# A list scheduler that prices each kind of small matrix product on its own, in a hybrid conformer, delta-net and feed-forward layer

## The chip, the cores and the metric

The kernel runs on one core of one Trainium2 chip. The metric is the device time of one execution in microseconds (us), less is better. A core has five engines that work side by side, each through its own instructions in a fixed order: TensorE (PE, matrix products into PSUM), VectorE (DVE), ScalarE (ACT), GpSimd (POOL) and SyncE (SP, which here issues all transfers).

## What is computed

The input has 512 tokens of width 1024, and 16 learned meta tokens go ahead of them. One layer and a last norm are computed, in float32:

```python
u = rmsnorm(h);  P = u @ w_in                       # one projection, columns shared out
c = silu(layernorm(causal_dwconv(c_val * sigmoid(c_gate), 31 taps)));  y_conf = c @ w_conf_out
q, k, v = silu(causal_dwconv(..., 4 taps)); q, k l2-normed    # 8 heads, width 128
o = chunk_gated_delta_rule(q, k, v, g, beta)        # state S per head, chunk by chunk
y_dn = (rmsnorm(o) * silu(z)) @ w_dn_out
h = h + (sigmoid(gA) * y_conf + sigmoid(gB) * y_dn) @ w_out
up = causal_dwconv(rmsnorm(h) @ w_up, 3 taps)
h = h + (silu(f_gate) * f_val) @ w_down             # d_ff 2816
return rmsnorm(h)[meta tokens dropped]
```

The delta rule needs, for each head and each chunk of 128 tokens, the inverse of a unit triangular 128x128 matrix.

## The kernel before

Features lie on partitions, tokens along the free dimension, in two halves of 258 or 264 columns. Each weight tile (wr, 128x1024) is split into a rounded part (wh, by ACT) and the rest (wl, by DVE), and so is each activation; a product of the full matrices is then three passes of fp32r products of 128x128 by 258, 264 or 512 columns. These are called big products here. A big product of 258 columns starts every 0.12 us.

Beside them stand small products in plain fp32, which the array takes as tiles of less than 128x128. The kinds are: 128x32 (`rs`, `sums`: sums over partitions, four token groups on four column groups), 32x32 and 64x64 (`gP` and `gX` in `grow`: the inverses of 32-blocks grow to 64 and 128), 32x128 and others for the 16 meta tokens. Full-width fp32 products of 128 columns do the chain of the state: `kS`, `wP`, `S` and `o`, four chunks per head in `heads`. Between these the chain runs over DVE (`r`, the new state `S`) and ACT (`w`).

DVE also does the 31-tap convolution of the conformer (`ca`, 240 steps) and the 32-block inverses; ACT empties most of PSUM.

No order is written out by hand. `record` notes every engine call with the tiles that it touches, and `Plan.order` puts the calls in a row: a list scheduler with a clock for each engine, which always takes the engine that can start first and gives it the ready call of the lowest number. The number is the place in the program, moved by `BIAS` and a few other constants for each stage. The time that a call is thought to take comes from `price`, the handover between engines from `LAT`. Each engine then keeps that order on the chip; where the planner's durations are off, an engine waits. Two lines matter most. A small product that does not begin at partition 0 of PSUM was priced at its issue alone, and leaving small products for others cost the number `STAY`, but only towards a product that is not small:

```python
            if out.ap.offset // out.tl.row:
                return 22, 0
...
                if e == "PE" and part and not o.part:
                    p += STAY
```

So the planner saw no cost in taking small products of different kinds in turn. Every recorded call carries one line in the profile, L427, since one helper issues all of them; groups are told apart by tile names.

Of the kernel before, what the change touches and what calls it, by code (L numbers as in the profile page):

```python
# [12 lines left out]
F32R = mybir.dt.float32r  # L13
# [6 lines left out]
P = 128  # L20
# [46 lines left out]
class Vw:  # L67
    """a view of a tile: the steps to it, and the same steps taken on a stand-in to know its bounds"""
# [52 lines left out]
class Op:  # L121
    _fields = ("eng", "fn", "a", "k", "prio", "deps", "succ", "late", "wait", "cost", "ready", "end", "tiles", "lat", "table")
# [11 lines left out]
TABLES = {'Exp': ('exp',), 'Tanh': ('exp', 'silu'), 'Silu': ('silu',), 'Sqrt': ('sqrt',)}  # L134
LAT = {'PE': {'PE': 3, 'DVE': 200, 'ACT': 200, 'POOL': 200, 'SP': 200},
# [5 lines left out]
WIN = 3413.3  # L141
LOW = 0.4
HIGH = 0.84
# ---- the order: how far ahead of the first open call each engine looks, slots kept for the tile that is next in
# line, what it costs to leave a run of small products or to change a function table ----
AHEAD = {'PE': 3000, 'DVE': 3000, 'ACT': 3000, 'POOL': 400, 'SP': 400}
KEEP = {"p1": 1, "st": 1, "bt": 2}
STAY = 3000
SWITCH = 600
# [1 line left out]
BIAS = {'k3': -850, 'iv': -1500, 'd0': 150, 'v4': -30, 'v2': 0, 'd7': 1500, 'z1': -320, 't11': -280, 'z5': 0, 't7': 250, 'k0': -250, 'ln': 250, 's7': 30, 'z0': -700, 'o2': -250, 'o5': 100, 'd5': -1850, 'g3': 150, 'd6': -250, 'd1': 2130, 'k2': -30, 'q7': -1720, 'k5': -30, 's4': -730, 'd4': 850, 'w3': -1600, 't2': -600, 'c5': -130, 't8': 60, 'v3': 250, 'o4': -600, 'q6': -250, 'g4': -350, 't4': -100, 'o1': 250, 'q4': -630, 't9': -150, 'z2': -600, 'o0': -600, 'g0': 30, 'q3': 250, 'q5': 700, 'c1': 30, 'c6': -130, 's1': 0, 't15': 200, 't1': -700, 's3': 100, 'y0': 250, 't12': -150, 'o6': 100, 'o3': 250, 'k4': -100, 'w2': 250, 't5': -250, 'v0': 30}  # L151
LNP = 74
IVP = 1265
UP = 519
WP = 144
# [39 lines left out]
class Plan:  # L195
# [18 lines left out]
    def add(self, eng, fn, a, k):  # L214
# [27 lines left out]
        o.part = eng == "PE" and fn == "matmul" and (writes[0].shape[0] < P or args[1].shape[0] < P) and writes[0].shape[0] % 32 == 0  # L242
        o.share = args[1].shape[0] / P if o.part else 1.0
        o.cost, o.lat = self.price(eng, fn, a, k, writes[0])
        if eng == "ACT" and fn == "activation":
            o.table = TABLES.get(str(k["func"]).split(".")[-1])
        self.ops.append(o)

    def price(self, eng, fn, a, k, out):
        n = out.n  # L250
        if eng == "PE":
            lhs, rhs = (k["lhsT"], k["rhs"]) if fn == "matmul" else (a[1], a[2])
            n = rhs.n
            if fn == "transpose":
                return 110, 0
            # a tile of the array beside one that is busy costs its issue alone
            if out.ap.offset // out.tl.row:
                return 22, 0
            return max(n, lhs.n) / 2.4 * (1 if lhs.tl.dt == F32R else 4) + 3, 0
        if fn == "dma_start":  # L260
            runs = [v.ap.ap[-1][1] if v.ap.ap[-1][0] == 1 else 1 for v in (k["out"], k["in_"])]
            return 475, int(np.prod(out.shape)) * 4 / 360.0 * (1 if min(runs) > 127 else 2)
# [3 lines left out]
        if eng == "ACT":  # L266
            return 0.833 * n + (51 if any(v.tl.space == "psum" for v in src) else 93) + 93 * aps + 93 * ("accum_out" in k), 0
        if eng == "DVE":
            r = {"reciprocal": 6.3, "tensor_copy": 1.04 if psum else 0.52, "tensor_scalar": 1.04 if psum else 0.52}.get(fn, 1.042)
            return r * n + 65 + 62 * aps, 0  # L270
        return 1.0 * n + 80, 0

    def order(self):
        """list scheduling: the engine that can start first takes its ready call of the lowest number"""
# [17 lines left out]
        part, drain = False, 0.0  # L292
        # a memset waits until the call that it is for has one other thing to wait for
# [13 lines left out]
        def look(e, t):  # L307
            """the call to take at t, or the next moment when there may be one"""
            q, nxt, best = ready[e], later[e][0][0] if later[e] else None, None
            for p, i in q:  # L310
# [23 lines left out]
                if e == "PE" and not o.part:  # L334
                    st = max(st, drain)
# [3 lines left out]
                if e == "PE" and part and not o.part:  # L339
                    p += STAY  # L340
                elif o.table and table not in o.table:
                    p += SWITCH
# [4 lines left out]
        while len(out) < len(ops):  # L347
# [26 lines left out]
            if e == "PE":  # L374
                # the tensor engine's clock: full after a busy window, half after an idle one
                while t >= (win + 1) * WIN:
# [4 lines left out]
                    win, act = win + 1, 0.0  # L381
                if cold:
                    c *= 2
                act += c * o.share
                part, drain = o.part, t + c + 86 if o.part else 0.0
            free[e] = t + c
            o.end = free[e]
            if e == "SP":
                dma = max(dma, t + 1100) + o.lat
                o.end = dma + 950  # L390
# [4 lines left out]
            for v in o.tiles:  # L395
# [4 lines left out]
                if not v.left and v.tag in slots:  # L400
                    heapq.heappush(slots[v.tag], tend[v] + 100)
            for j in o.succ:
                s = ops[j]
                s.ready = max(s.ready, o.end + LAT[e][s.eng])
# [25 lines left out]
def record(A, out):  # L430
# [41 lines left out]
    def weights(src, n=D):  # L472
        """raw tile -> its 12-bit part and the exact rest"""
# [9 lines left out]
    def gemm(acc, ws, ah, al, ranges, k0=0, kn=None, first=True, last=True):  # L483
# [3 lines left out]
        if ah is uh and WHOLE:  # L487
            # not before all of its rows are there: it would hold its banks
# [12 lines left out]
    def sums(ss, width):  # L501
        """tiles [128, width]: sum over tiles and partitions, four token groups on partition groups"""
# [8 lines left out]
    def spread(r, width, n):  # L511
        """such rows on every partition of a tile in SBUF"""
# [9 lines left out]
    def rstd_rows(ss, width, scale, bias):  # L522
        """the sums' 1/sqrt(scale*sum+bias)"""
# [19 lines left out]
    # the first products take the input without its norm's scale, which comes after them  # L543
# [3 lines left out]
    # products of nothing while the first loads run: the tensor engine's clock is up when they are in  # L547
# [34 lines left out]
    # 32 columns: four k-tiles at a time, side by side in the array; their sums come with the turn to tokens  # L582
# [38 lines left out]
    # halves of the products below come doubled out of (tanh + 1)  # L621
# [35 lines left out]
    # beta = exp(min(b, 0)) / (1 + exp(-|b|))  # L657
# [9 lines left out]
    # cumulated decays: by token on partitions, by row, and the chunks' totals  # L667
# [47 lines left out]
    def conv4(acc, t, way=None):  # L715
        """four causal taps, then silu; from PSUM [128, 2, 268], or [128, 2, 264] moved out first, or SBUF"""
# [37 lines left out]
    def decays(h):  # L754
        """E[j, i] = exp(gc_i - gc_j) for j <= i, else 0"""
# [9 lines left out]
    def grams(h):  # L765
# [23 lines left out]
        # b = beta / (|k|^2 + eps)  # L789
# [22 lines left out]
    def inverses():  # L812
# [478 lines left out]
```

## Time and profile before

| | |
|---|---|
| median of 3 runs | 1048.68 us (1046.71 to 1049.07) |
| span of the profiled execution | 1049.7 us |
| PE busy | 1035.5 us, 99% |
| DVE busy | 718.3 us, 68% |
| ACT busy | 474.7 us, 45% |
| mean granted clock of PE | 0.985 of full |

The span reaches from the first to the last instruction of one profiled execution; what lies around it has no row, and the span is 1.0 us above the median of the runs. PE's busy share is high because its queue is rarely empty: a busy PE may still be working through products that are slow for their size, so the table alone doesn't tell how much time could go. The granted clock is 1.00 at 2.4 GHz and 0.50 at 1.2 GHz.

### The profile page before, as it was taken

Reading aid. Unit: us, or ns where it says so; the run is one execution under the profiler, and the core shown is the slowest. Engines: PE = TensorE matmul, PEld = TensorE weight load, DVE = VectorE, ACT = ScalarE, POOL = GpSimd, SP = SyncE. Lnnn points to the kernel's source line nnn. Section 1 sums busy time; section 2 is a strip of 40 time slices with the busy share of each in tenths; the row PEclk is TensorE's granted clock in tenths of the full one; section 3 lists DMA queues with packets and bytes.
Section 4 is the critical chain, followed back from the end, with each engine's and each line's share of the span. In section 5 each row is a group of like instructions: output and inputs, shape, how many; then the busy total and the mean of one; then the engine's idle time right before and its main releaser. Section 6 shows DMA issues by size and latency. Waiting matters only on the chain.

```text
span 1049.7 us, 20033 instructions
## 1 busy us (share of the span) xinstructions
PE 1035.5 (99%) x8430; PEld 985.7 (94%) x8430; DVE 718.3 (68%) x1237; ACT 474.7 (45%) x863; POOL 9.5 (1%) x45
## 2 busy tenths in 40 slices
PE   9999999999999999999999999999999999999996
PEld 7999999988989999999999999999999999988885
DVE  6987899984867998985546555666666767623324
ACT  6777622557534466444345234534444443413222
POOL 0011000000000000000000000000000000000000
PEclk9999999987999999999999999999999999999998
DMA  6244323231211232212313343232323232333232
GB/s 223 76 123 110 114 82 111 81 102 42 71 42 61 81 106 98 78 65 76 127 61 122 101 143 99 81 102 81 100 81 101 81 101 81 96 91 91 81 105 81
DMA packets 44042, 98.40 MB, mean 94 GB/s; under 512 B 12720, under 2 KB 19248, under 8 KB 43952
## 3 DMA queue, kind: packets, MB, share of 16 engines
q1 hardware_dynamic: 43952, 97.12, 29.2%
q8 instruction: 66, 1.08, 0.4%
q14 instruction: 24, 0.20, 0.1%
HBM read 93.89 MB, written 3.21 MB: 93 GB/s over the span
## 4 chain that ended last, share of the span: by engine, by line
PE 96%; DVE 1%; ACT 1%; DMA 0%; SPq 0%; issue 0%; POOL 0%; DVEq 0%; POOLq 0%; ACTq 0%
PE up L427 24%; PE dn L427 12%; PE ga L427 9%; PE y L427 9%; PE k L427 5%; PE v L427 5%; PE z L427 5%; PE q L427 4%; PE wo L427 4%; PE cv L427 4%; PE cg L427 4%; PE rs L427 2%; PE o L427 2%; PE gX L427 1%; PE S L427 1%; PE gP L427 1%
## 5 line engine op out<-in xcount | busy, mean ns | idle before, releaser
L427 DVE TENSOR_TENSOR wl<-wr,wh 128x1024 fp32r<-128x1024 f32 x157 | 189.3, 1207 | 160.1 <-PE dn L427 47.8
L427 ACT CAST wh<-wr 128x1024 fp32r<-128x1024 f32 x157 | 162.0, 1037 | 287.5 <-PE up L427 87.8
L427 DVE SCALAR_TENSOR_TENSOR ca<-c,par,ca 128x516 f32<-128x516 f32 (+10 forms) x240 | 177.3, 744 | 7.3 <-ACT ca L427 4.8
L427 PE MATMUL up<-hl,wh 128*128 128x258 f32 x704 | 142.1, 283 | 0.0
L427 PE MATMUL up<-hh,wh 128*128 128x258 f32 x704 | 142.1, 283 | 0.0
L427 PEld LDWEIGHTS up<-hh,wh 128*128 128x128 f32 x704 | 109.0, 190 | 0.2 <-issue 0.2
L427 PEld LDWEIGHTS up<-hl,wh 128*128 128x128 f32 x704 | 108.9, 189 | 0.0
L427 PE MATMUL up<-hh,wl 128*128 128x258 f32 x704 | 92.4, 283 | 0.0
L427 PEld LDWEIGHTS up<-hh,wl 128*128 128x128 f32 x704 | 88.3, 189 | 0.0
L427 DVE TENSOR_TENSOR up<-up,r 128x258 f32<-128x258 f32 x88 | 33.4, 420 | 49.0 <-PE up L427 46.0
L427 DVE SCALAR_TENSOR_TENSOR uy<-up,par,uy 128x512 f32<-128x512 f32 x88 | 65.9, 748 | 1.5
L427 PE MATMUL dn<-fh,wh 128*128 128x512 f32 (+1 forms) x198 | 65.0, 369 | 0.0
L427 PE MATMUL dn<-fl,wh 128*128 128x512 f32 (+1 forms) x198 | 64.9, 369 | 0.0
L427 ACT ACTIVATE uy<-up,par 128x512 f32<-128x512 f32 x44 | 36.0, 817 | 53.8 <-DVE up L427 53.8
L427 PE MATMUL ga<-uh,wh 128*128 128x258 f32 x256 | 58.5, 290 | 0.0
L427 PE MATMUL ga<-ul,wh 128*128 128x258 f32 x256 | 57.9, 289 | 0.0
L427 DVE SCALAR_TENSOR_TENSOR cv<-ra,par,cv 128x528 f32<-128x528 f32 x69 | 51.6, 760 | 0.6 <-ACT cv L427 0.5
L427 PE MATMUL dn<-fh,wl 128*128 128x512 f32 (+1 forms) x198 | 49.8, 370 | 0.0
L427 PE MATMUL ga<-uh,wl 128*128 128x258 f32 x256 | 48.4, 299 | 0.0
L427 PEld LDWEIGHTS dn<-fh,wh 128*128 128x128 f32 x198 | 36.9, 188 | 7.8 <-ACT wh L427 1.2
L427 PEld LDWEIGHTS dn<-fl,wh 128*128 128x128 f32 x198 | 36.9, 188 | 6.9
L427 PEld LDWEIGHTS ga<-ul,wh 128*128 128x128 f32 x256 | 42.2, 189 | 0.8 <-issue 0.6
(284 smaller groups left out, 2238.9 us busy)
## 6 DMA issues: line engine op xcount, KB each, us to landing
wr<-in_win SPq DMA_DIRECT2D x64, 512.0 KB, 3.3
wr<-in_wup SPq DMA_DIRECT2D x44, 512.0 KB, 3.7
wr<-in_wd SPq DMA_DIRECT2D x17, 512.0 KB, 3.6
wr<-in_wdn SPq DMA_DIRECT2D x8, 512.0 KB, 3.2
wr<-in_wco SPq DMA_DIRECT2D x8, 512.0 KB, 3.4
wr<-in_wo SPq DMA_DIRECT2D x8, 512.0 KB, 3.3
wr<-in_wd SPq DMA_DIRECT2D x8, 384.0 KB, 3.1
x<-in_xT SPq DMA_DIRECT2D x8, 264.0 KB, 5.8
```

The costliest lines, as they stand in the source:

```text
L427: getattr(engines[o.eng], o.fn)(*(get(x) for x in o.a), **{n: get(x) for n, x in o.k.items()})
```

## The change

The mathematics and the set of calls stay as they are; 7720 products on PE in both. What changes is the planner. A small product now has a kind (`mode`, rows by columns of the tile that it takes of the array). It pays `TURN` when the kind changes, in either direction and between two small kinds, and then its full cost as well. Leaving a kind costs `STAY` in number towards every other kind. Durations in `price` are new for most operations, transfers are thought slower, and what small products count for in the planner's own bookkeeping of PE's clock is new. `BIAS`, `LNP`, `IVP`, `WP` and `SWITCH` have other values, so the whole order is another. Comments are gone. The core of the diff:

```diff
-STAY = 3000
-SWITCH = 600
+STAY = 4687.5
+SWITCH = 300
...
+RATE = 0.4453
+TURN = {(False, True): 92, (True, False): 105, (True, True): 190}
...
-        o.part = eng == "PE" and fn == "matmul" and (writes[0].shape[0] < P or args[1].shape[0] < P) and writes[0].shape[0] % 32 == 0
+        o.mode = None
+        if eng == "PE" and fn == "matmul":
...
+            up = lambda n: 32 if n <= 32 else 64 if n <= 64 else P
+            o.mode = (up(args[1].shape[0]), up(writes[0].shape[0]))
+            o.mode = None if o.mode == (P, P) else o.mode
...
+        o.alone = self.price(eng, fn, a, k, writes[0], True)[0] if o.mode else o.cost
...
-            return max(n, lhs.n) / 2.4 * (1 if lhs.tl.dt == F32R else 4) + 3, 0
+            if lhs.tl.dt == F32R:
...
+                return RATE * n + 4 + (2 if rhs.ap.offset % rhs.tl.row % 4 else 0), 0
+            if lhs.shape[0] == 64:
+                return 115, 0
+            return max(n, lhs.n) / 0.6 + 8, 0
...
-                if e == "PE" and part and not o.part:
+                if e == "PE" and mode and o.mode != mode:
                     p += STAY
...
+                if o.mode != mode:
+                    c = o.alone + TURN[bool(mode), bool(o.mode)]
```

First place: PE in the middle of the delta rule, where `grow` for later heads and the head norms' sums come together (`gX` and `gP` are products of `grow`, `rs` with `hsel` are the sums of a head's squares `o` and `q`; `o_3`, `S_3` are products for the meta tokens). Before:

```order
L427 MATMUL S_3_3811<-w_6_3801,kdm_930 128x128
L427 MATMUL o_3_3813<-Em_1000,w_6_3801 128x16
L427 MATMUL gX_3817<-DU_2902,gp_3805 32x32
L427 MATMUL rs_3819<-o_1_3454,hsel_71 32x129
L427 MATMUL gX_3817<-DU_2902,gp_3805 32x32
L427 MATMUL rs_3819<-o_1_3454,hsel_71 32x129
L427 MATMUL gX_3817<-gp_3805,DU_2902 32x32
```

The same sums with the change:

```order
L447 MATMUL ga_3869<-uh_117,wl_3846 128x258 x2
L447 MATMUL ga_3869<-uh_125,wl_3846 128x258 x2
L447 MATMUL rs_3999<-o_1_3389,hsel_71 32x129 x4
L447 MATMUL rs_3999<-q_1_2775,hsel_71 32x129 x4
L447 MATMUL rs_3999<-o_2_3691,hsel_71 32x129 x4
L447 MATMUL rs_3999<-q_3_3632,hsel_71 32x129 x4
L447 MATMUL wP_4020<-r_9_3992,mn_1263 128x128
```

The sums stand in one run of 16 behind big products, and the products of `grow` in runs of their own elsewhere.

Second place: PE where the growth of the inverses begins (`ga` and `q` are big products). Before:

```order
L427 MATMUL ga_2915<-ul_121,wh_2850 128x258
L427 MATMUL gP_3002<-LL_2950,mn_1351 32x32 x5
L427 MATMUL gX_3028<-DU_2902,gp_3013 32x32
L427 MATMUL gP_3002<-LL_2950,mn_1351 32x32
L427 MATMUL gX_3028<-DU_2902,gp_3013 32x32
```

With the change:

```order
L447 MATMUL gP_2937<-LL_2912,mn_1225 32x32 x7
L447 MATMUL q_2947<-uh_93,wh_2845 128x264 x2
L447 MATMUL q_2947<-ul_95,wh_2845 128x264 x2
L447 MATMUL q_2947<-uh_97,wh_2845 128x264
L447 MATMUL gP_2983<-LL_2918,mn_1341 32x32 x8
L447 MATMUL q_2947<-uh_97,wh_2845 128x264
L447 MATMUL gX_2998<-DU_2843,gp_2977 32x32 x2
```

More big products stand between the first steps of the growth.

Third place: DVE at the end of the program (`fin` are output tiles, eight for each half of the tokens, `rr` is the norm's reciprocal, `xr` with `dn` the last residual). Before:

```order
L427 TENSOR_TENSOR fin_11675<-xr_7450,rb_11655 128x256
L427 TENSOR_TENSOR fin_11679<-xr_7452,rb_11655 128x256
L427 TENSOR_TENSOR fin_11679<-xr_7497,rb_11655 128x256
L427 RECIPROCAL rr_11668<-rr_11668 128x64
L427 TENSOR_TENSOR fin_11690<-xr_7020,rb_11685 128x256
```

With the change:

```order
L447 TENSOR_TENSOR fin_11653<-xr_7448,rb_11614 128x256
L447 TENSOR_TENSOR fin_11653<-xr_7496,rb_11614 128x256
L447 TENSOR_TENSOR xr_7496<-xr_7496,dn_11573 128x256
L447 RECIPROCAL rr_11682<-rr_11682 128x64
L447 TENSOR_TENSOR fin_11690<-xr_7322,rb_11685 128x256
```

The first half's eight output tiles now stand ahead of the last residual, and nothing stands between it and the second half's reciprocal. On PE 38 big products stand between the first half's `rb` and the end, where none stood.

## Rows read from the trace of the kernel before

**Rows 1.** The page: the span, and the chain that ended last by engine.

```profile
span 1049.7 us, 20033 instructions
...
PE 96%; DVE 1%; ACT 1%; DMA 0%; SPq 0%; issue 0%; POOL 0%; DVEq 0%; POOLq 0%; ACTq 0%
```

**Rows 2.** Windows: stretch, busy PE, PEld, DVE, ACT, POOL; granted clock; DMA.

```profile
98.00:112.00 14.00, 11.98 (x97) 11.20 (x96) 11.76 (x32) 11.54 (x52) 1.51 (x4) 1.00 0.46 97
112.00:224.00 112.00, 112.00 (x919) 110.96 (x919) 103.90 (x244) 41.59 (x68) 0.98 (x5) 1.00 0.34 103
224.00:263.00 39.00, 37.77 (x451) 33.43 (x450) 22.32 (x39) 28.59 (x89) 0.34 (x2) 0.74 0.15 42
...
484.70:1036.70 552.00, 552.00 (x4261) 528.06 (x4260) 303.93 (x425) 213.81 (x275) 0.00 (x0) 1.00 0.29 93
1036.70:1049.67 12.97, 3.24 (x25) 2.84 (x24) 6.36 (x18) 1.14 (x3) 0.00 (x0) 0.61 0.47 162
```

**Rows 3.** PE's timeline from 290.5 us: start, duration, instruction, records (two per fp32 product).

```profile
291.14 0.24 PE L427 MATMUL gX<-DU,gp 32*32 32x32 f32 x2
...
291.65 0.24 PE L427 MATMUL gX<-DU,gp 32*32 32x32 f32 x2
...
299.56 0.39 PE L427 MATMUL z<-uh,wh 128*128 128x258 f32 x1
```

**Rows 4.** PE's timeline from 319.2 us.

```profile
319.36 0.33 PE L427 MATMUL gP<-LL,mn 64*64 64x64 f32 x2
...
324.08 0.52 PE L427 MATMUL q<-uh,wh 128*128 128x264 f32 x2
```

**Rows 5.** The chain that ended last: start, time on it, what, records.

```profile
227.66 0.57 PE gX L427 x32
...
229.14 0.60 PE gP L427 x8
...
376.13 0.58 PE rs L427 x16
...
484.75 2.14 PE rs L427 x72
```

**Rows 6.** Timeline of the last 20 us, all engines.

```profile
1036.67 1.08 PE L427 MATMUL rb<-rr,cst 128*128 128x64 f32 x8
...
1037.78 2.74 DVE L427 TENSOR_TENSOR fin<-xr,rb 128x256 f32<-128x256 f32 x8 [0.60 <-PE rb L427]
1038.08 0.31 ACT L427 ACTIVATE rr<-rs,eps 128x64 f32<-128x64 f32 x1
...
1040.44 0.55 DVE L427 RECIPROCAL rr<-rr 128x64 f32<-128x64 f32 x1
1041.13 1.94 PE L427 MATMUL rb<-rr,cst 128*128 128x64 f32 x8 [3.13 <-DVE rr L427]
```

**Rows 7.** The chain that ended last, from 94 to 112 us.

```profile
98.82 5.04 DMA E<-d_g
```

**Rows 8.** Windows of 10 us in the growth of the inverses, columns as in rows 2.

```profile
230.00:240.00 10.00, 9.81 (x95) 8.50 (x96) 3.74 (x6) 6.37 (x21) 0.00 (x0) 0.53 0.13 44
...
250.00:260.00 10.00, 9.67 (x121) 8.27 (x120) 3.85 (x7) 8.25 (x27) 0.34 (x2) 0.73 0.13 29
```

**Rows 9.** PE's timeline from 362.2 us, one link of the state's chain.

```profile
362.37 0.38 PE L427 MATMUL kS<-S,cv 128*128 128x128 f32 x2
362.58 0.39 PE L427 MATMUL o<-cv,S 128*128 128x128 f32 x2
362.73 0.37 PE L427 MATMUL q<-uh,wh 128*128 128x264 f32 x1
362.93 0.41 PE L427 MATMUL q<-ul,wh 128*128 128x264 f32 x2
...
363.42 0.38 PE L427 MATMUL wP<-r,mn 128*128 128x128 f32 x2
```

**Rows 10.** Groups of instructions: the convolution's taps on DVE.

```profile
L427 DVE SCALAR_TENSOR_TENSOR ca<-c,par,ca 128x516 f32<-128x516 f32 x96 | 71.8, 748 | 5.2 <-ACT ca L427 4.8
```

More of the change, by code (lines that the diff above doesn't have):

```diff
@@ L121 @@
 class Op:
-    _fields = ("eng", "fn", "a", "k", "prio", "deps", "succ", "late", "wait", "cost", "ready", "end", "tiles", "lat", "table")
+    _fields = ("eng", "fn", "a", "k", "prio", "deps", "succ", "late", "wait", "cost", "ready", "end", "tiles", "lat", "table", "mode", "act", "tail", "alone")
 class Rec:
@@ L134 @@
 TABLES = {'Exp': ('exp',), 'Tanh': ('exp', 'silu'), 'Silu': ('silu',), 'Sqrt': ('sqrt',)}
-LAT = {'PE': {'PE': 3, 'DVE': 200, 'ACT': 200, 'POOL': 200, 'SP': 200},
+LAT = {'PE': {'PE': 0, 'DVE': 200, 'ACT': 200, 'POOL': 200, 'SP': 200},
        'DVE': {'PE': 300, 'DVE': 127, 'ACT': 130, 'POOL': 130, 'SP': 130},
@@ L141 @@
 WIN = 3413.3
-LOW = 0.4
+RATE = 0.4453
+TURN = {(False, True): 92, (True, False): 105, (True, True): 190}
+LOW = 0.5
 HIGH = 0.84
@@ L241, in add @@
         o.deps, o.succ, o.table = deps, [], None
-        o.part = eng == "PE" and fn == "matmul" and (writes[0].shape[0] < P or args[1].shape[0] < P) and writes[0].shape[0] % 32 == 0
-        o.share = args[1].shape[0] / P if o.part else 1.0
+        o.mode = None
[3 more added lines that the diff above has]
+            o.mode = None if o.mode == (P, P) else o.mode
         o.cost, o.lat = self.price(eng, fn, a, k, writes[0])
+        o.alone = self.price(eng, fn, a, k, writes[0], True)[0] if o.mode else o.cost
+        o.act = (args[2].n if writes[0] is args[0] else args[1].n) / 0.6 * o.mode[0] / P if o.mode else o.cost
+        o.tail = 950 + (2800 if fn == "dma_start" and o.lat > 700 and self.run(k) <= P else 0)
         if eng == "ACT" and fn == "activation":
@@ L247, in add, with run, price @@
         self.ops.append(o)
-    def price(self, eng, fn, a, k, out):
+    @staticmethod
+    def run(k):
+        return min(v.ap.ap[-1][1] if v.ap.ap[-1][0] == 1 else 1 for v in (k["out"], k["in_"]))
+    def price(self, eng, fn, a, k, out, alone=False):
         n = out.n
@@ L255, in price @@
                 return 110, 0
-            if out.ap.offset // out.tl.row:
+            if out.ap.offset // out.tl.row and not alone:
                 return 22, 0
-            return max(n, lhs.n) / 2.4 * (1 if lhs.tl.dt == F32R else 4) + 3, 0
+            if lhs.tl.dt == F32R:
[3 more added lines that the diff above has]
+            return max(n, lhs.n) / 0.6 + 8, 0
         if fn == "dma_start":
-            runs = [v.ap.ap[-1][1] if v.ap.ap[-1][0] == 1 else 1 for v in (k["out"], k["in_"])]
-            return 475, int(np.prod(out.shape)) * 4 / 360.0 * (1 if min(runs) > 127 else 2)
+            return 475, int(np.prod(out.shape)) * 4 / 290.0 * (1 if self.run(k) >= P else 2)
         aps = sum(isinstance(k.get(x), Vw) for x in ("scalar", "scalar1", "scalar2", "scale", "bias", "mul"))
@@ L266, in price @@
         if eng == "ACT":
-            return 0.833 * n + (51 if any(v.tl.space == "psum" for v in src) else 93) + 93 * aps + 93 * ("accum_out" in k), 0
+            return 0.833 * n + (51 if any(v.tl.space == "psum" for v in src) else 93) + 93 * aps + 93 * ("accum_out" in k) + (124 if out.shape[0] in (32, 64) else 0), 0
         if eng == "DVE":
             r = {"reciprocal": 6.3, "tensor_copy": 1.04 if psum else 0.52, "tensor_scalar": 1.04 if psum else 0.52}.get(fn, 1.042)
-            return r * n + 65 + 62 * aps, 0
+            return r * n + 65 + 62 * aps + (134 if fn == "transpose" else 0), 0
         return 1.0 * n + 80, 0
@@ L291, in order @@
         win, act, cold = 0, 0.0, True
-        part, drain = False, 0.0
+        mode = None
         for i, o in enumerate(ops):
@@ L333, in look @@
                     continue
-                if e == "PE" and not o.part:
-                    st = max(st, drain)
                 if st > t:
@@ L381, in order @@
                     win, act = win + 1, 0.0
+                if o.mode != mode:
+                    c = o.alone + TURN[bool(mode), bool(o.mode)]
                 if cold:
                     c *= 2
-                act += c * o.share
-                part, drain = o.part, t + c + 86 if o.part else 0.0
+                act += o.act * (2 if cold else 1)
+                mode = o.mode
             free[e] = t + c
@@ L388, in order @@
             if e == "SP":
-                dma = max(dma, t + 1100) + o.lat
-                o.end = dma + 950
+                dma = max(dma, t + 950) + o.lat
+                o.end = dma + o.tail
             out.append(i)
@@ L401, in order @@
                     heapq.heappush(slots[v.tag], tend[v] + 100)
+            drain = 110 if o.mode else 0
             for j in o.succ:
                 s = ops[j]
-                s.ready = max(s.ready, o.end + LAT[e][s.eng])
+                s.ready = max(s.ready, o.end + LAT[e][s.eng] + (drain if s.eng != e else 0))
                 s.wait -= 1
```

8 lines of the change are left out of this document (4 added, 4 removed).

## The prediction, made before the changed kernel was run

> **What bounds the kernel now.** I read the page first. PE holds 96% of the chain that ended last in a span of 1049.7 us [rows 1], so time can only be won by making PE's own queue shorter, by letting it wait less, by keeping its clock up, or behind its last product. The windows by stretch come next [rows 2]. From 484.7 to 1036.7 us PE is busy throughout at full clock with the big products of the output projections and the feed-forward part. The change removes none of these, so 552 us stay. The stretch from 112 to 224 us is full as well. What is left to win lies in four places.
>
> The first is hidden behind a full busy time and shows only in the timeline [rows 3, 4]. From 291.14 us PE takes a product of `grow` and a product of the norm's sums in turn, and a pair takes 291.65 - 291.14 = 0.51 us, though each is tiny. There are 16 such pairs and four more `gP` before the next big product at 299.56 us, so 8.42 us. From 319.36 to 324.08 us the same happens with 8 pairs (four with 64x64 products, four with 32x32) and 8 more `gX`: 4.72 us. Together that is 13.14 us. The second place is the growth of the inverses, 224 to 263 us: PE is busy for 37.77 of 39 us, but at a mean granted clock of 0.74 [rows 2], 0.53 in its worst 10 us [rows 8]. The third is a real wait, 14.00 - 11.98 = 2.02 us from 98 to 112 us [rows 2]. The fourth is the end, where PE works 3.24 us of 12.97 [rows 2].
>
> **The change part by part.** *Runs of one kind.* The changed order has no pair left of `rs` and `gX` or `gP` in turn: the 24 sums stand in runs of 16 and 8, the products of `grow` that stood beside them in runs of 8 to 24. What they cost in runs is in the chain [rows 5], where a small product has two records: 8 `rs` take 0.58 us, 36 take 2.14; 16 `gX` of 32x32 take 0.57; four `gP` of 64x64 take 0.60. The two stretches hold 24 `rs` (24 x 0.58 / 8 = 1.74 us), 32 products of 32x32 (32 x 0.57 / 16 = 1.14) and four of 64x64 (0.60), so 3.48 us. The gain is 13.14 - 3.48 = 9.7 us. By the long run, 2.14 / 36 a sum, it would be 10.0; if the runs were broken once each, about 9.
>
> The Trainium skill speaks against this gain in "TensorEngine Tiling (Array Packing)", Key Properties: tiles operate independently, and different tiles can load weights and multiply in parallel. By that alone a 32x32 and a 128x32 product in turn would overlap, this gain would be nothing and the sum 9.7 us longer, about 1044. The same list says that changing the mode drains the engine, by which the gain stands. The pair's 0.51 us against 0.07 + 0.04 us in runs [rows 3, 5] sides with the second sentence.
>
> *Changes of kind elsewhere.* Counted in the two orders, PE changes kind 226 times before and 184 times after. The two stretches alone hold 48 of the 226, so elsewhere there are 6 more. One change costs (0.51 - 0.11) / 2 = 0.2 us by the pairs [rows 3, 5], so 1.2 us are given back.
>
> *Full-width small products.* They too are bunched more (`kS`, `gg` and `qk` follow each other directly). That costs nothing: `kS` ahead of `o` takes 0.21 us, `o` ahead of a big product 0.15 us, and then that big product 0.20 us in place of 0.12 [rows 9], so 0.23 us for the second one as well.
>
> *The end.* Before, the second half's reciprocal starts at 1040.44 us though its square root was done at 1038.08 + 0.31 = 1038.39; it stands behind eight `fin` of the first half (2.74 us) on DVE [rows 6]. With the change these `fin` run beside 38 big products (38 x 0.12 = 4.6 us, so they are covered with 1.8 us to spare). That takes off 1040.44 - 1038.39 = 2.0 us. The last `rb` took 1.94 us where the first took 1.08 [rows 6], the clock being lower by then (0.61 over the last stretch [rows 2]); started 2 us sooner it may keep the full clock, up to 0.9 us more. I take 2.4, bounds 2.0 and 2.9.
>
> *The wait at 98 to 112 us.* It hangs on the transfer of `E`, 5.04 us [rows 7]: ACT's exponentials of `E` stand ahead of the reads that free PSUM for the next `gg`. In the changed order 96 big products stand between the two halves of one head's `gg`, 11.5 us of cover, but two weight casts on ACT now stand behind the last two `E`. I take half the wait, 1.0 us, bounds 0 and 2.
>
> *The growth of the inverses.* At 0.74 over 39 us, 39 x 0.26 = 10.1 us of clock are lost [rows 2]. What came before the drop was PE in runs of tiny products: in the order of before only 10 big products stand among the first 56 of the 224 products of `gP` and `gX`, and 39 among the first 112; with the change it is 23 and 46. That is denser, though not by much, and the dependent steps (product, copy on ACT, product) are as many as ever. The bounds are 0 (the clock falls as before) and 10.1 (it holds). The numbers of big products are nearer to the old, so I take 4.
>
> *New waits.* The changed order leaves 5 or 6 big products between `kS` and `wP` where mostly 6 to 11 stood. That is enough where DVE is free: at 362.37 us five big products and one `o` filled the link exactly, 1.05 us from `kS` to `wP` [rows 9]. But no row shows the new order's waits. Bounds are 0 and 6 us (three waits as at 98 to 112 us); I take 1, since the link in rows 9 is the nearest.
>
> The sum against the profiled execution: 1049.7 - 9.7 + 1.2 - 2.4 - 1.0 - 4.0 + 1.0 = 1034.8 us. The span lies 1.0 us above the median of the runs, 1048.68, so the runs should come to 1033.8, say 1034.
>
> **The rivals.** *The clock holds.* If the denser start of the growth keeps the clock at 1.00, the term is 10.1 in place of 4, and the time is about 1028 (1024 to 1029). For it: 23 big products in place of 10 at the start. Against it: the stretch of before fell twice, and the second fall came among links of the state's chain, which still stand there.
>
> *The copies become the bound.* A run of products of `grow` ends sooner, but each step waits for ACT to move PSUM into SBUF, and ACT is already busy for 28.59 of these 39 us [rows 2]. PE has a fixed order, so it would stand still where it used to work slowly. Then the growth takes as long as before (4 us given back) and each later piece of growth that lost its slow neighbour waits too, up to 6 us: 1038 to 1045. Against it: in the changed order the steps of those later pieces stand 90 and more big products apart, over 10 us. The Trainium skill has this as a rule, in "TensorEngine Tiling (Array Packing)", PSUM Bottleneck: tiling speeds up TensorE but not the evacuation of PSUM, which may become the bottleneck. By that rule the time would be this rival's; in the rows ACT has 10 of the 39 us free, so the trace bears it out in part only.
>
> *Slower: taps between the links.* The state's chain passes DVE 56 times (32 `r`, 24 new states), and on DVE 240 taps of 0.748 us [rows 10] wait their turn. With 5 big products of cover, nothing is left over for a tap that happens to stand ahead. DVE was 103.90 of 112 us busy before the growth [rows 2], so work that is late there is pushed into the chain's stretch. If a link waits 0.37 us on average, half a tap, that is 56 x 0.37 = 20.7 us, more than all the gain: about 1055. It decides from 14.9 / 56 = 0.27 us a link. Against it: the link in rows 9 shows no wait at all with five products of cover.
>
> *No change.* The ends of PE's products are modelled in a profile, so the pairs could be cheaper than they look and overlap, with something else holding PE. Without the 9.7 us, and with the clock's 4 lost in the same way, the runs come to 1047.5, no change that can be told. The first of the two sentences from the Trainium skill would have it so for the pairs. Against it: starts are recorded, and the next big product does not start until 8.42 us later [rows 3].
>
> **How the numbers follow.** My forecast (1029 to 1039) has 0.55, the clock that holds 0.17, the copies 0.15, no change 0.05, slower 0.08. The range 1025 to 1045 takes in the forecast, and nearly all of the two cases beside it. A measurement of this kernel can tell about 0.2% from no change, 2.1 us; only the last two cases are not faster by more than that. So faster has 0.87, the same 0.05, slower 0.08.
>
> **What would show it.** No alternation of `rs` with `gX` or `gP` in PE's timeline, and a run of 16 `rs` in 1.0 to 1.2 us, show the first term right. At the end, the reciprocal should start within 0.1 us of its square root, with the eight `fin` beside big products. The window around the growth should show a mean clock between 0.8 and 0.95; under 0.75 means that the term of 4 is lost, and 1.00 that it is too small. Idle time of PE before `wP` or `S` that names DVE would be the slower rival, before `gX` naming ACT the copies. I am wrong if the middle part, up to the first `wo`, is not shorter by 10 us or more, or if the part from there to the last big product changes by over 2 us.

## The result, and the profile of the changed kernel

The changed kernel takes 1037.84 us (median of 4 runs, 1036.56 to 1038.69), the kernel before 1047.7 us on the same chip (4 runs, 1046.06 to 1049.07). The ratio is 0.9894, with a 95% interval of 0.9871 to 0.9917: faster by 0.8 to 1.3%. The profiled execution took 1037.39 us. Its span is 14.1 us shorter than that of before, more than the 9.9 us between the medians; the section on the prediction comes back to this.

First the page: the span, and the chain that ended last by engine. These answer to [rows 1].

```profile
span 1035.6 us, 20040 instructions
...
PE 93%; DVE 4%; ACT 2%; DMA 1%; issue 0%; DVEq 0%; ACTq 0%; SPq 0%
```

PE still sets the end, but 7% of the chain now run over other engines, 4% of it over DVE, where it was 1%, which points to a new wait of PE's. The windows show where (columns as in [rows 2]; the last one begins behind the last big product, as it did there).

```profile
70.00:80.00 10.00, 7.40 (x55) 7.01 (x54) 5.37 (x16) 6.07 (x12) 3.54 (x4) 0.89 0.61 176
...
98.00:112.00 14.00, 13.46 (x114) 12.70 (x113) 8.87 (x31) 12.16 (x58) 2.40 (x2) 1.00 0.36 73
112.00:224.00 112.00, 111.94 (x916) 110.83 (x915) 104.03 (x246) 43.86 (x77) 2.08 (x8) 1.00 0.34 109
224.00:263.00 39.00, 39.00 (x538) 35.02 (x538) 28.65 (x50) 31.79 (x100) 0.48 (x3) 1.00 0.17 57
...
1024.60:1035.60 11.00, 2.26 (x16) 1.94 (x16) 3.71 (x10) 1.14 (x3) 0.00 (x0) 0.60 0.29 98
```

Between 224 and 263 us PE issues 538 records at a granted clock of 1.00, where it issued 451 at 0.74 [rows 2]. From 98 to 112 us it stands still for 0.54 us instead of 2.02. But from 70 to 80 us it loses 2.6 us, and the mean clock falls to 0.89, in a stretch where 0.15 us was lost before and the clock stayed at 1.00.

PE's timeline at the run of sums that took turns with the growth's products [rows 3]:

```profile
303.33 0.43 PE L447 MATMUL rs<-o,hsel 128*32 128x129 f32 x8
303.58 0.40 PE L447 MATMUL rs<-q,hsel 128*32 128x129 f32 x8
303.80 0.40 PE L447 MATMUL rs<-o,hsel 128*32 128x129 f32 x8
304.02 0.40 PE L447 MATMUL rs<-q,hsel 128*32 128x129 f32 x8
304.35 0.49 PE L447 MATMUL wP<-r,mn 128*128 128x128 f32 x2
```

Sixteen `rs` (32 records) are over in 304.35 - 303.33 = 1.02 us, 0.064 us each. In turns each of them came with a product of the growth and the two took 0.51 us.

The chain that ended last, from 68 us (start, time on it, what, records):

```profile
68.56 6.13 DMA Em<-d_gm
74.69 0.03 issue
74.71 1.62 DVE Em L447 x8
...
77.98 0.14 DVE Mm L447
78.12 0.04 issue
78.17 1.12 PE kt L447 x4
```

This is the new loss. A transfer of 8 KB takes 6.13 us of the chain, DVE (and ACT with it) waits for it, and PE waits 2.60 us at 78.17 for the bank of PSUM that DVE's `Mm` empties. From 77.8 us, when PE still waits, to 81.3 the clock is at half. The half clock doesn't come with the wait each time: in the profiled executions of e2_after_alternate and e7_dense (below) PE waits 2.39 and 2.25 us at this place and the clock stays at 1.00.

The end, all engines, answering to [rows 6]:

```profile
1019.01 1.00 PE L447 MATMUL rb<-rr,cst 128*128 128x64 f32 x8
...
1020.05 2.73 DVE L447 TENSOR_TENSOR fin<-xr,rb 128x256 f32<-128x256 f32 x8
...
1023.46 1.12 PE L447 MATMUL dn<-fh,wl 128*128 128x256 f32 x8
...
1025.93 0.31 ACT L447 ACTIVATE rr<-rs,eps 128x64 f32<-128x64 f32 x1
1026.27 0.55 DVE L447 RECIPROCAL rr<-rr 128x64 f32<-128x64 f32 x1 [1.24 <-ACT rr L447]
1026.97 1.94 PE L447 MATMUL rb<-rr,cst 128*128 128x64 f32 x8 [1.11 <-DVE rr L447]
```

The eight `fin` run beside big products, and the reciprocal starts 0.03 us behind its square root, where it came 2.05 us late. From the end of the last big product (1024.58) to the end of the span it is 11.0 us in place of 12.95. The last `rb` takes 1.94 us as it did: the clock had fallen at 1026.7 all the same. And the first `rb`, which lay behind the last big product before [rows 6], now stands between big ones.

### The profile page after: what moved, and what is told of

The parts are those of the page before. It is cut to its first block, busy times and chain, and to the rows that moved or that the text cites. A ratio compares the mean times of both kernels' runs of the same rounds, so it can differ in the third digit from the quotient of the medians.

```text
span 1035.6 us, 20040 instructions
## 1 busy us (share of the span) xinstructions
PE 1021.4 (99%) x8430; PEld 977.3 (94%) x8430; DVE 716.9 (69%) x1237; ACT 479.5 (46%) x867; POOL 10.8 (1%) x45
## 4 chain that ended last, share of the span: by engine, by line
PE 93%; DVE 4%; ACT 2%; DMA 1%; issue 0%; DVEq 0%; ACTq 0%; SPq 0%
PE up L447 25%; PE dn L447 12%; PE ga L447 9%; PE y L447 8%; PE v L447 5%; PE q L447 5%; PE z L447 5%; PE cv L447 5%; PE wo L447 4%; PE cg L447 4%; PE o L447 2%; PE k L447 1%; PE rs L447 1%; DVE cv L447 1%; PE S L447 1%; PE wP L447 1%
## 5 line engine op out<-in xcount | busy, mean ns | idle before, releaser
L447 DVE SCALAR_TENSOR_TENSOR ca<-c,par,ca 128x516 f32<-128x516 f32 (+15 forms) x240 | 176.0, 744 | 2.5
L447 PE MATMUL dn<-fh,wh 128*128 128x512 f32 (+1 forms) x198 | 71.9, 371 | 0.0
L447 PE MATMUL dn<-fl,wh 128*128 128x512 f32 (+1 forms) x198 | 71.4, 369 | 0.0
L447 PE MATMUL dn<-fh,wl 128*128 128x512 f32 (+1 forms) x198 | 45.3, 369 | 0.0
L447 PE MATMUL ga<-uh,wl 128*128 128x258 f32 x256 | 45.3, 287 | 0.0
```

The costliest lines, as they stand in the source:

```text
L447: getattr(engines[o.eng], o.fn)(*(get(x) for x in o.a), **{n: get(x) for n, x in o.k.items()})
```

## The experiments

Each experiment lets the planner make its order and then rearranges one engine's row of calls. A helper puts the five rows together again, so that each call follows what it depends on and no more buffers are open than there are. Where a big product was moved so far that ACT or DVE would have held it up, these two may pass a call that isn't ready (said where it is so). Times are medians; the ratio is to the kernel before on the same chip, with its 95% interval; the clock is the median over the runs.

| run | us (lowest to highest, runs) | ratio | clock |
|---|---|---|---|
| changed kernel | 1037.84 (1036.56 to 1038.69, 4) | 0.9894 (0.9871 to 0.9917) | 0.994 |
| e1_before_grouped | 1037.63 (1034.26 to 1041.86, 6) | 0.9895 (0.9873 to 0.9917) | 0.991 |
| e2_after_alternate | 1047.59 (1046.76 to 1049.72, 11) | 0.9992 (0.998 to 1.0004) | 0.997 |
| e3_before_sparse | 1048.91 (1048.09 to 1053.1, 12) | 1.0003 (0.9991 to 1.0015) | 0.991 |
| e4_after_kt_later | 1038.2 (1035.93 to 1039.33, 5) | 0.9891 (0.9874 to 0.9907) | 0.994 |
| e5_em_first | 1034.05 (1033.5 to 1034.63, 5) | 0.9859 (0.9835 to 0.9883) | 0.997 |
| e6_spaced | 1038.06 (1037.79 to 1038.75, 6) | 0.9898 (0.9876 to 0.992) | 0.995 |
| e7_dense | 1044.87 (1035.99 to 1049.14, 12) | 0.9955 (0.9928 to 0.9983) | 0.987 |
| e8_tail | 1035.69 (1034.99 to 1037.11, 5) | 0.9875 (0.9847 to 0.9902) | 0.996 |
| e9_both | 1033.63 (1033.09 to 1033.8, 4) | 0.9849 (0.9827 to 0.9871) | 0.997 |
| e10_singles | 1049.07 (1048.15 to 1049.72, 12) | 0.9999 (0.9986 to 1.0011) | 0.996 |

The kernel before ran 57 times beside them: 1048.66 us, 1044.02 to 1053.2, at clocks from 0.996 to 0.984, median 0.989.

**The turns alone, taken out of the kernel before.**

```diff
+    for a, b in ((2156, 2192), (2338, 2362)):        # PE's row, the two stretches
+        pe[a:b] = sorted(pe[a:b], key=lambda i: plan.ops[i].tiles[0].name == "rs")
```

> The kernel before with one edit: in the two stretches at 291 and 319 us where sums (rs) and products of the growth (gX, gP) take turns, the same products stand grouped, the growth's first and the 16 and 8 rs behind them. Nothing else moves on any engine. Theory (the turns themselves are the price): the 13.1 us of the two stretches become 16 rs and 8 rs in 1.0 and 0.5 us and the growth's products in about 1.5 us, so the time falls by 9 to 10 us, from 1047.7 to about 1038. Rival (the turns were spent in time in which PE had to wait for copies anyway): PE waits at the products behind the stretches instead, the time falls by less than 3 us.

It took 11.0 us less, as much as the whole change. PE's timeline at the two stretches, to be read beside [rows 3] and [rows 4]:

```profile
287.44 0.22 PE L465 MATMUL gX<-DU,gp 32*32 32x32 f32 x2
...
287.97 0.32 PE L465 MATMUL rs<-o,hsel 128*32 128x129 f32 x4
...
288.99 0.38 PE L465 MATMUL z<-uh,wh 128*128 128x258 f32 x1
...
308.79 0.67 PE L465 MATMUL gP<-LL,mn 64*64 64x64 f32 x8
...
310.35 0.51 PE L465 MATMUL q<-uh,wh 128*128 128x264 f32 x2
```

8.42 us became 1.55, and 4.72 became 1.56: 10.0 us together. No wait of PE over 0.25 us appeared behind either. The remaining microsecond is in the scatter of the clock: at a clock of 0.996 this kernel took 1034.26 us and the kernel before 1044.02. The theory holds, its rival falls.

**The turns alone, put back into the changed kernel.**

```diff
+    part = pe[2293:2454]
+    rs = [i for i in part if name(i) == "rs"]        # 16 and 8
+    gx = [i for i in part if name(i) == "gX"]        # 24
+    rest = [i for i in part if i not in rs and i not in gx]
+    pe[2293:2454] = rest + [i for pair in zip(gx, rs) for i in pair]
```

> The changed kernel with one edit: 24 of its rs (a run of 16 and one of 8) are moved behind to its run of 24 gX and take turns with them; 43 changes of kind more, nothing else moves. Theory (turns are the price): a pair took 0.51 us in the kernel before, grouped the two take about 0.09 us, so 24 pairs add 10 us: from 1037.8 to about 1048. Rival (the price was in what stood around the turns before): under 3 us more.

9.75 us more than the changed kernel, where 10 were expected. That it fits to a quarter of a microsecond is in part chance: its median clock is 0.997 where the changed kernel has 0.994, and from the first `gP` to the first `y` its profiled execution takes 10.6 us more, 0.54 of it in a new wait of `kS` for DVE. Its PE timeline, the first two pairs and what follows the 24th:

```profile
319.13 0.24 PE L482 MATMUL gX<-DU,gp 32*32 32x32 f32 x2
319.31 0.41 PE L482 MATMUL rs<-o,hsel 128*32 128x129 f32 x2
319.64 0.24 PE L482 MATMUL gX<-DU,gp 32*32 32x32 f32 x2
319.82 0.41 PE L482 MATMUL rs<-o,hsel 128*32 128x129 f32 x2
...
331.39 0.51 PE L482 MATMUL v<-uh,wh 128*128 128x264 f32 x2
```

12.26 us for 24 pairs, 0.51 us a pair to the hundredth, in another place of the program beside other work. So the price belongs to the turns. What also follows: the changed kernel with turns (1047.59) is the kernel before again, within 0.2%. All the rest of the new order together comes to nothing between these medians (at clocks of 0.997 and 0.989), though not for want of effects, as the next runs show.

**Is it the turn of two small kinds, or any change of kind?**

```diff
+    big = rest[-49:]                                 # rest: the part without rs, as above, to 2504
+    pe[2293:2504] = rest[:-49] + [i for n in range(24) for i in (rs[n], big[2 * n], big[2 * n + 1])] + big[48:]
```

> The changed kernel with one edit: the same 24 rs as in the run with turns, each by itself between big products, one behind every second one, so that no small product stands next to another kind of small one; 44 changes of kind more, all between a small product and a big one. Theory (each change of kind has its price, 0.2 us, whichever two kinds they are, as the prediction's 1.2 us for six changes took it): 9 to 10 us more than the changed kernel, about 1047. Rival (turns of two small kinds are the dear ones, beside big products a change is mostly covered by the weights that are loaded ahead): 2 to 6 us more.

11.2 us more for 44 changes of kind, 0.25 us each if all of it is put down to them (`kS`, near where the sums stood before, now waits 0.55 us for DVE). PE's timeline shows one period:

```profile
320.47 0.41 PE L482 MATMUL rs<-o,hsel 128*32 128x129 f32 x2
320.81 0.39 PE L482 MATMUL v<-uh,wh 128*128 128x264 f32 x1
321.04 0.28 PE L482 MATMUL v<-ul,wh 128*128 128x264 f32 x1
321.25 0.41 PE L482 MATMUL rs<-o,hsel 128*32 128x129 f32 x2
```

A sum and two big products take 321.25 - 320.47 = 0.78 us. In a run the sum takes 0.064, and two big products 0.24; the two changes cost the other 0.47, so 0.23 us each, beside a big product as well as beside a small one. The theory holds; big products don't cover a change. The Trainium skill says in "TensorEngine Tiling (Array Packing)", Key Properties, that changing the mode drains TensorE; the trace agrees, with 0.23 us a change here and 0.21 in turns. (In a run of the changed kernel 24 `gX` take 0.63 us, 0.026 each, so a pair in turns has (0.51 - 0.064 - 0.026) / 2 = 0.21 us for each change.)

**The growth of the inverses.** Two runs exchange how closely big products are strewn among the first 100 small ones. The edit moves big products only: ahead of the k-th small product stand as many as in the other kernel (`max` draws them forward in the kernel before, `min` puts them behind in the changed one).

```diff
+    for k, i in enumerate(small):                    # small and big: PE's row from the first gP on
+        want = max(was[k], at[k]) if k < len(at) else was[k]
+        res += big[ahead:max(ahead, want)]
+        ahead = max(ahead, want)
+        res.append(i)
```

> The kernel before with one edit: over the first 100 small products of the growth (224 to 234 us) big products are drawn forward, so that as many stand ahead of each small one as in the changed kernel, 13 more by the 100th at most; 9 changes of kind are added. Theory (big products in between keep the clock up): of the 13.7 us at half clock from 230.6 us most run at full clock, 4 to 7 us less, less 1.8 us for the changes of kind, so 2 to 5 us less in all and a granted clock over 0.8 in the stretch. Rival (the clock falls for the small products themselves, however they lie, or the stretch is bound by its copies): the clock still stands at 0.5 for 10 us or more, and the time is the same or 2 us more.

The time stayed: 1048.91 to 1048.66, with 9 changes of kind more (9 x 0.23 = 2.1 us) and 17 rows of ACT's queue in other places. The window of the growth in its profile:

```profile
224.00:263.00 39.00, 37.92 (x473) 33.09 (x472) 22.57 (x40) 29.68 (x93) 0.34 (x2) 0.82 0.13 42
```

and in that of the first experiment, whose order is that of before up to 287 us:

```profile
224.00:263.00 39.00, 37.45 (x491) 33.36 (x490) 24.67 (x44) 30.87 (x96) 0.34 (x2) 0.87 0.14 42
```

The clock of 0.82 is above the 0.74 of before [rows 2], but below the 0.87 that the unchanged order reached in another execution. So this run says nothing either way. The second run is the reverse, in the changed kernel:

> The changed kernel with one edit: over the first 100 small products of the growth only as many big products stand ahead of each as in the kernel before, 11 fewer by the 100th; they follow behind it. Kinds change as often as in the changed kernel (182 for 184). Theory (fewer big products in between let the clock fall): a granted clock near 0.5 for some 7 to 14 us behind 230 us and 3 to 7 us more than the changed kernel. Rival (how the big products lie there doesn't set the clock): the clock stays at 1.00 or falls for under 4 us, and the time is within 2 us of the changed kernel.

The median rose by 7.0 us, and the runs fall into groups by their clock: six of 12 at 0.982 or 0.983 took 1047.95 to 1049.14 us, four at 0.991 took 1040.89 to 1041.79, one at 0.994 1039.69, one at 0.997 1035.99. Windows of the profiled one (1048.85 us):

```profile
230.00:240.00 10.00, 10.00 (x76) 8.46 (x74) 6.60 (x9) 3.25 (x12) 0.00 (x0) 0.50 0.08 27
240.00:250.00 10.00, 10.00 (x86) 8.76 (x86) 4.55 (x8) 5.16 (x17) 0.00 (x0) 0.50 0.01 2
250.00:260.00 10.00, 10.00 (x87) 9.45 (x87) 4.46 (x9) 6.07 (x16) 0.00 (x0) 0.65 0.25 81
```

The clock stands at half from 229.7 to 257.0 us, and PE issues 76 records in 10 us. The edit does less than the expectation says: fewer big products stand ahead of the first 72 small ones only (at most 13 fewer, 10 in place of 23 ahead of the 50th), and from the 73rd on, at 238.3 us, PE's order is that of the changed kernel. From there to 257.0 PE is busy all the time at 0.50 with an order that ran at 1.00 in the changed kernel. So up to 13 big products put a little later decide whether the clock falls, and not in each execution. The theory holds in this direction: the new order's closer weave keeps the clock up in the growth, and none of the 52 runs of versions that keep it was under 0.993. Two things stay open. That the same weave would have kept the clock up in the kernel before isn't shown, as the run ahead of this one says nothing. And short waits come with the looser order, 0.71 us at 229.4 us for ACT's `mn` in this run, where the changed kernel has none over 0.25 us in its growth; no run tells the two apart.

**The new wait at 78 us.** Three edits of the changed kernel. First, the waiting `kt` behind the big products that follow it:

```diff
+    pe[500:525] = pe[504:525] + pe[500:504]
```

> The changed kernel with one edit: the four kt that wait 2.6 us at 78 us for a bank of PSUM that DVE's Mm frees, and behind them the clock at half, are put behind the 21 big products that follow them. Theory (the wait and the low clock behind it are a loss of the new order and need not be): 2.6 us of wait and 1.7 us of half clock go, so 3 to 4.5 us less than the changed kernel, about 1033.5. Rival (the late work only passes its delay on: kd, the Gram products gg and the masks behind kt come as late as they do now and PE waits there): within 1 us of the changed kernel.

No gain; the wait only moved on, as the rival had it. PE's timeline:

```profile
78.58 0.66 PE L485 MATMUL kt<-cst,cv 128*128 128x128 f32 x4 [0.37 <-DVE Mm L485]
82.36 0.28 PE L485 MATMUL ktm<-cst,cv 128*16 128x128 f32 x1 [3.13 <-ACT junk L485]
```

Then `kt` and all that came behind it put further back, behind 21 and 29 big products (8 rows of DVE's and 21 of ACT's queue change places too):

```diff
+    kt, ktm, gg, kt2 = pe[500:504], pe[525:526], pe[534:539], pe[540:544]
+    big = pe[504:525] + pe[526:534] + pe[539:540] + pe[544:564]
+    pe[500:564] = big[:21] + kt + big[21:50] + ktm + gg + kt2
```

> The changed kernel with one edit: kt is put behind 21 big products as in the run before, and what waited then in its place, ktm with the Gram products and the next kt, behind 29 more. Theory (PE has big products enough to cover both waits, and nothing behind is short of time): no wait over 0.5 us between 70 and 90 us and no low clock there, 3 to 4.5 us less than the changed kernel. Rival (the chain over ScalarE and VectorE only gets later, the growth starts as late): the wait goes, but the first product of the growth or the chain of the state waits instead, and the time stays within 1 us.

No gain either, though neither for the reason of the theory nor of the rival: the big products now wait themselves, `cg` for its accumulators, 3.54 us.

```profile
82.77 0.48 PE L482 MATMUL cg<-uh,wh 128*128 128x264 f32 x2 [3.54 <-DVE nb L482]
```

Neither of these two orders of PE helps, since DVE and ACT are late all the same. The third edit goes to the cause, on SP's queue:

```diff
+    em = next(n for n, i in enumerate(sp) if names(i) == ["Em", "d_gm"])
+    e = next(n for n, i in enumerate(sp) if names(i) == ["E", "d_g"])
+    sp.insert(e, sp.pop(em))
```

> The changed kernel with one edit: on SP's queue the small transfer of the masks' rows for the meta tokens (Em from d_gm) is issued ahead of the two first of the token masks (E from d_g) instead of behind them, so that it isn't queued in their 5 us. Theory (VectorE and ScalarE stand still from 71 to 74.7 us for this transfer, and the wait of kt for Mm and the low clock follow from it): Em lands near 71, the wait of 2.6 us at kt and the half clock of 3.4 us go, 3 to 4.5 us less than the changed kernel. Rival (the masks E, now a microsecond later, are what the Gram products' banks wait for, or the transfer takes its 5 us wherever it stands): within 1 us of the changed kernel, or slower.

3.8 us less than the changed kernel, and no run of the one reaches into the range of the other. They ran on different chips; `e6_spaced`, which ran on the chip of this run, took 1037.79 us or more. The tile `Em` in this trace, PE's `kt`, and the window:

```profile
DMA to landing us min/median/max: 1.7/1.7/1.7
```

```profile
75.28 0.64 PE L482 MATMUL kt<-cst,cv 128*128 128x128 f32 x4
...
79.05 0.28 PE L482 MATMUL ktm<-cst,cv 128*16 128x128 f32 x1 [0.55 <-ACT junk L482]
```

```profile
70.00:80.00 10.00, 9.45 (x78) 9.03 (x77) 7.29 (x22) 9.43 (x28) 3.49 (x4) 1.00 0.79 224
```

Ahead of the two masks `E` the same 8 KB land in 1.7 us instead of 6.13; `kt` doesn't wait, and the clock stays at 1.00. The masks are 256 KB each. The Trainium skill says in "DMA: Bandwidth & Descriptors", Queues, rings and completion order, that each DMA engine takes its descriptors in ring order; by that rule a small transfer behind two large ones has theirs ahead of it, and the trace agrees (6.13 us against 1.7). The planner counts 2 us for it alone (0.95 to issue, 0.06 for the bytes, 0.95 behind them) and at most 0.9 more for each mask ahead of it. In the kernel before, `Em` stood behind one mask (issued at 69.59 us) and was used no sooner, at 74.6 us, but DVE and PE had other work at hand, as its window shows:

```profile
70.00:80.00 10.00, 9.85 (x80) 9.23 (x79) 9.32 (x25) 8.68 (x22) 3.20 (x4) 1.00 0.73 198
```

**The end.**

```diff
+    pe[n:n + 42] = pe[n + 4:n + 42] + rb             # rb of the first half, behind the last big product
+    ve[n:n + 10] = [xr] + fin[:2] + [rr] + fin[2:]   # DVE: the second reciprocal behind two of eight fin
```

> The changed kernel with one edit at the end: the four rb of the first half of the tokens stand behind the last big product instead of 38 ahead of it, and the second reciprocal stands behind two of the first half's eight fin. Theory (where they stand now the four rb take 0.8 us from the big products, behind the last one they lie beside the chain over xr, fsq and its sums): 0.6 to 0.8 us less between the last but one stage and the end, read from the profile; the total moves by less than its uncertainty. Rival (the first half's fin and transfers come so late that the end waits for them): the time from the last big product to the end grows from 11.0 to 12 us or more, and the total is the same or up to 1 us more.

The timeline of the end:

```profile
1022.26 1.12 PE L482 MATMUL dn<-fh,wl 128*128 128x256 f32 x8
1023.21 1.00 PE L482 MATMUL rb<-rr,cst 128*128 128x64 f32 x8
...
1025.07 0.55 DVE L482 RECIPROCAL rr<-rr 128x64 f32<-128x64 f32 x1
1025.54 4.66 DVE L482 TENSOR_TENSOR fin<-xr,rb 128x256 f32<-128x256 f32 x14
1025.77 1.08 PE L482 MATMUL rb<-rr,cst 128*128 128x64 f32 x8 [1.11 <-DVE rr L482]
```

The first `rb` lies beside the chain over `xr`, `fsq` and `rs` again, and from the last big product (1023.38) to the end (1034.3) it is 10.9 us, so nothing is lost there. The 0.8 us that `rb` took among big products are won: from the first `dn` to the end of the last it is 124.07 us in place of 124.97. The median fell by 2.1 us, more than the end explains; its runs had a clock of 0.996 where those of the changed kernel had 0.994. The second `rb` kept the full clock here.

**Both together**, the version that the runs point to:

> The changed kernel with the two edits that were worth something: Em's transfer ahead of the masks E, and at the end rb of the first half behind the last big product with the second reciprocal behind two fin. Theory (the two lie 900 us apart and their gains add): 3.8 + 0.5 to 2 us less than the changed kernel, 1032 to 1033.5, the fastest of all. Rival (one of the two gains was the luck of its executions' clock): no faster than the run with Em alone, about 1034.

1033.63 us, the fastest of all, 1.5% under the kernel before (interval 1.3 to 1.7%) and 4.2 us under the changed kernel. The end adds 0.4 us to the transfer's gain; the runs of the two overlap at 1033.5 to 1033.8, so that part isn't shown by the time alone.

## Why the prediction was right, and where its steps were off

The time of 1037.84 us lies 3.8 us above the 1034 and in the likeliest case's own range; faster it is. By its steps:

- **Runs of one kind, -9.7.** Right in mechanism and in size: 10.0 us by the rows of the first experiment, 9.75 by the medians of the second. That PE's price is in the turns was the one step on which nearly everything hung, and it was read from starts in the timeline where the busy share said 99%.
- **Changes of kind elsewhere, +1.2.** Right in the price: 0.2 us a change was taken over from pairs of small products, and the singles show 0.23 beside big ones. The number was too high: the first experiment, grouped only, still has 181 changes, so 3 of the 6 belong to the runs whose cost the first term already holds, and 0.7 us is left. Counted over the whole program (226 to 184), 42 changes at 0.23 are 9.7 us, for both terms together (9.7 - 1.2 = 8.5 in the prediction).
- **The end, -2.4, bounds 2.0 and 2.9.** Mis-sized. The stall of the reciprocal went as said (2.02 us sooner), but the last `rb` didn't keep the clock, and what I had not priced is the first `rb`: behind the last big product it had been hidden, and ahead of it its slot costs 1019.82 - 1019.01 = 0.8 us (the next `dn` starts at 1019.82). That leaves 1.2.
- **The wait at 98 to 112 us, -1.0.** 1.5 of its 2.02 us went.
- **The growth's clock, -4.0, bounds 0 and 10.1.** Mis-sized against the profiled execution: the window's clock is 1.00, which I had named as the sign that the term is too small. 39 x 0.26 = 10.1 us of clock came back, but not all of it is time. A line through the 57 runs of the kernel before gives 0.76 us for each 0.001 of the mean clock, where a thousandth of the span is 1.05 us; so 10.1 of clock are about 7.3 us of time. Measured on the runs it is less again. The profiled execution of before had a clock of 0.985, near the lowest of the 57. Runs are 1.8 us longer than their spans, so it stands for a run of about 1051.5 us (an estimate), 2.8 above the median, where I had taken 1.0 off its span. Against the median clock of 0.989, the changed kernel's 0.994 are worth 0.005 / 0.001 x 0.76 = 3.8 us, with the half clock at 78 us already taken off; without that it is about 5 (an estimate). My term of 4 is about right for the median, and I made the sum against an execution in which it is 7.
- **New waits, +1.0, bounds 0 and 6.** Mis-sized and looked for in the wrong place. The chain of the state has no wait over 0.25 us (the slower rival's 56 links cost nothing, and no `gX` waits for ACT either). The waits came at 61 us (0.44) and 78 us (2.60) with 1.7 us of half clock behind them: 4.7. I had looked at what the new order does to products on PE, and not at which transfer stands ahead of which on SP and how bare DVE's row is while it waits (5.37 of 10 us busy from 70 to 80).

With the measured sizes the sum is 1049.7 - 10.0 + 0.7 (three changes of kind more than in the first experiment) - 1.2 - 1.5 - 7.3 + 4.7 = 1035.1, for a span of 1035.6. It leaves out 39.00 - 37.77 = 1.23 us of PE's waits in the growth, which went, and a new wait of 0.37 us of `y` for DVE at 533 us; with both it is 1034.2, and 1.4 us stay open. The terms that were off, -3.3 in the growth, +3.7 in new waits, +1.2 at the end and -0.5 at 98 us, took each other back. That the forecast lies within 4 us is therefore in part luck; that the kernel is faster rests on the first term.

Of the rivals, the clock held, yet its 1028 did not come: its saving went into the wait at 78 us, and the clock is not worth its full time. No change falls with the second experiment, the copies with the window at 224 to 263 us, where PE is busy 39.00 of 39. Of the two signs of being wrong neither came: up to the first `wo` it is 12.8 us less, and from there to the end of the last big product the time changed by +0.7 us, that `rb`. The chain has the first `wo` here, for the kernel before, where its last big product ended at 1035.60 + 1.12:

```profile
609.90 46.10 PE wo L427 x384
```

and here for the changed one, with its end at 1023.46 + 1.12:

```profile
597.06 46.30 PE wo L447 x384
```

What stays open: why one and the same order runs at clocks from 0.984 to 0.996. The first experiment's stretch up to 287 us is that of before call by call, and its clock in the growth was 0.87 against 0.74.

## What to carry to other kernels

A busy PE is not a working PE: look at the distance between starts in its timeline, and count how often the array changes its tile size. Here each change costs 0.21 to 0.23 us by the rows, beside big products too, and grouping 36 small products and 24 sums without touching anything else was worth the whole change. When an order is computed anew, look for new losses where the planner's prices are wrong. Here the largest was a transfer queued behind two large ones, and it was mended on the queue that feeds the waiting engines; moving the waiting products only passed the wait on, both times.

## What the hardware showed beyond what was expected

- The granted clock differs between executions of one program (0.984 to 0.996 over 57 runs of the kernel before), and the time goes with it: 1053.2 us at 0.984, 1044.02 at 0.996. Two kernels are compared best at one clock, and a single profiled execution can be 3 us of clock away from the median (0.985 against 0.989, at 0.76 us for each 0.001).
- Up to 13 big products fewer ahead of the first 72 small ones of the growth moved the median by 7 us, and the same program then ran in groups at clocks of 0.983 and 0.991, with single runs at 0.994 and 0.997. In the profiled execution the clock stayed at half for 18.7 us more in an order that ran at full clock where it was reached at full clock.
- A change of tile size costs about the same between two small sizes (32x32 and 128x32, 0.21 us) and between a small one and the full array (128x32, 0.23 us). Each is the mean of a change and the change back; the two directions were not measured apart.
- An 8 KB transfer took 6.13 us (on the chain) behind two of 256 KB and 1.7 us ahead of them.
